# Transposes in the middle of a slice's matmuls, half of each cast of b on VectorE, and a last output piece of 128 columns: what each did to matmul, GELU, matmul

## The chip, the cores and the metric

One core of one Trainium2 chip. The metric is the device time of the whole program in microseconds (us). It holds about 1.8 us that the profiled span doesn't (before: 124.75 us for a span of 123.0 us).

## The reference

```python
h = a @ b                       # a 1024 x 1024, b 1024 x 2048, fp32
h = 0.5 * h * (1 + tanh(sqrt(2 / pi) * (h + 0.044715 * h**3)))
return h @ c                    # c 2048 x 1024
```

## The kernel before

The contraction of the first product runs over k in eight slices of 128. In the opening, six groups of 128 columns of b (the first 768 columns of the tile b_lo; GpSimd loads its other 512 for the next four groups) are multiplied with the first 512 rows of a, slice by slice as the data land. SyncE issues those loads. VectorE (DVE) casts a slice of a to bf16, TensorE (PE) transposes it, DVE copies it out of PSUM, ScalarE (ACT) casts the slice of b.

```python
    nc.gpsimd.tensor_copy(gate, b_st[5][:, 0:1])    # GpSimd waits for b slice 5 before its own loads
    ...
    def mm0(k):
        for t in range(N0):                                   # N0 = 6
            nc.tensor.matmul(ps[t], bt(k, t), aT[0][:, k, :], ...)

    for k in range(KT):                                       # KT = 8
        ab = abf.tile([128, 4, 128], BF16, name="ab")
        nc.vector.tensor_copy(ab, a_st[k])                    # cast of a
        pt = tpool.tile([128, H], BF16, name="pt")
        for j in range(4):
            nc.tensor.transpose(pt[:, ts(j, 128)], ab[:, j, :], ident)
        nc.vector.tensor_copy(aT[0][:, k, :], pt)             # copy of aT
        for i in range(2):
            nc.scalar.activation(b_lo[:, k, ts(i, W0 // 2)], b_st[k][:, ts(i, W0 // 2)], AF.Copy)
        if k > 0:
            mm0(k - 1)                                        # one slice behind the transposes
    mm0(KT - 1)
    ...
    for k in range(0, KT, 4):                                 # the next four column groups
        load_b(k, 4, W0, W1)                                  # GpSimd loads and casts them
        for i in range(4):
            for t in range(N1):
                nc.tensor.matmul(ps[t], bt(k + i, N0 + t), aT[0][:, k + i, :], ...)
    ... # (cut: the rest of both products)
    for q in range(2):                                        # last output row block, two pieces of 256
        w = H // 2
        p = bank(w)
        prod(p, whole(h12), whole(c21), 3, q=ds(q * w, w))
        ot = new_out()
        nc.vector.tensor_tensor(ot[:, 0:w], p, last_keep[:, ds(q * w, w)], op=ADD)
        store(ot, 3, q * w, w)
```

## Time and profile before

124.86 us median of 4 runs (124.63 to 124.98).

| stretch of the profiled run | what sets its end |
|---|---|
| 0 to 17.1 us | landing of a and b |
| 17.1 to 22.1 us | PE: two slices' transposes, three slices' matmuls; and a GpSimd load landing at the same moment |
| 22.1 to 119.6 us | PE, nearly without a gap |
| 119.6 us to the end | an addition, a store of 128 KB, the closing |

The same opening by stretch, from the profile before. The columns are the stretch, its length, then busy us and number of instructions of PE, PE's weight loads, DVE, ACT and GpSimd, the granted clock, the DMA engines' busy share and GB/s.

```profile
10.00:17.00 7.00, 5.99 (x38) 3.07 (x40) 3.22 (x8) 3.75 (x8) 1.33 (x3) 1.00 1.06 378
17.00:22.10 5.10, 4.75 (x28) 2.08 (x27) 1.93 (x4) 2.79 (x6) 4.46 (x7) 1.00 1.12 194
```

DVE is busy for less than half of these stretches and ACT for about half.

### The profile page before, as it was taken

The page shows a single profiled execution, that of the slowest core. Times are in us where ns is not written, and L with a number is a line of the kernel's source. Part 1 is how long each engine was busy: PE and PEld are TensorE (multiplying, and loading weights), DVE is VectorE, ACT ScalarE, POOL GpSimd, SP SyncE. Part 2 cuts the span into 40 slices and gives each one's busy share as a digit, 9 for nine tenths or more (in the row PEclk, how much of TensorE's full clock was granted, in tenths as well). Part 3 has the DMA queues.
Part 4 walks back from the last instruction along what each step waited for, and adds up shares of the span by engine and source line. Part 5 has one row for each costly group of instructions (what it writes and reads, how often), then busy time and mean ns, then how long its engine had stood idle before and what let it go on. Part 6 is the DMA issues. An engine that isn't in the chain of part 4 may idle for free.

```text
span 123.0 us, 1436 instructions
## 1 busy us (share of the span) xinstructions
PE 114.0 (93%) x555; PEld 66.8 (54%) x562; DVE 65.2 (53%) x94; ACT 29.6 (24%) x54; POOL 21.1 (17%) x26
## 2 busy tenths in 40 slices
PE   6955889999998999999999999999999999999990
PEld 2323444444456444444444444468888888888860
DVE  0233533000015200007999999999669999964440
ACT  4034545806331133233323333000000000000000
POOL 2000099133440210000000000995000000000000
PEclk9999999999999999999999999999999999999997
DMA  3899999999999999996000000001500023353433
GB/s 108 198 358 384 379 295 193 205 202 203 212 206 206 316 398 238 206 208 103 0 3 0 5 0 0 0 0 55 201 0 0 5 85 113 143 195 146 171 143 113
DMA packets 14213, 18.43 MB, mean 150 GB/s; under 512 B 768, under 2 KB 9728, under 8 KB 14208
## 3 DMA queue, kind: packets, MB, share of 16 engines
q0 software_dynamic: 7968, 8.91, 39.4%
q1 hardware_dynamic: 6240, 9.44, 22.0%
q8 instruction: 4, 0.07, 0.2%
q14 instruction: 1, 0.01, 0.0%
HBM read 20.97 MB, written 4.19 MB: 205 GB/s over the span
## 4 chain that ended last, share of the span: by engine, by line
PE 82%; DMA 12%; DVE 1%; SPq 1%; issue 1%; DVEq 0%
PE ps L246 41%; PE ps L143 31%; DMA a_st<-in_a_dram 12%; PE ps L102 3%; PE ps L134 3%; PE pt L134 3%; PE pt L162 1%; DVE aT L163 1%; PE pt L110 1%; DVE ab L107 0%; SPq L82 0%; SPq L76 0%; DVE ot L316 0%; DVEq L107 0%
## 5 line engine op out<-in xcount | busy, mean ns | idle before, releaser
L119 ACT ACTIVATE h<-ps 128x512 fp32r<-128x512 f32 (+1 forms) x30 | 17.3, 602 | 27.5 <-PE ps L143 25.2
L143 PE MATMUL ps<-aT,b_hi 128*128 128x512 bf16 x93 | 21.2, 379 | 0.2
L143 PE MATMUL ps<-aT,b_lo 128*128 128x512 bf16 x79 | 17.4, 379 | 0.1
L143 PEld LDWEIGHTS <-b_hi 128*128 128x128 bf16 x96 | 9.3, 98 | 10.8
L246 PE MATMUL ps<-t,s 128*128 128x512 f32 x64 | 15.1, 393 | 0.0
L246 PE MATMUL ps<-t,h 128*128 128x512 f32 x64 | 14.8, 389 | 0.0
L246 PE MATMUL ps<-c,h 128*128 128x512 bf16 (+1 forms) x71 | 14.1, 355 | 0.1
L246 PEld LDWEIGHTS ps<-t,s 128*128 128x128 f32 x64 | 12.0, 188 | 2.6
L246 PEld LDWEIGHTS ps<-t,h 128*128 128x128 f32 x64 | 12.0, 188 | 2.5
L286 POOL COPY lk<-u 128x512 f32<-128x512 f32 x1 | 7.6, 7579 | 33.5 <-ACT u L279 33.5
L143 PEld LDWEIGHTS <-b_lo 128*128 128x128 bf16 x80 | 7.8, 98 | 9.4
L200 DVE TENSOR_TENSOR t<-c,c 128x1024 fp32r<-128x1024 bf16 x4 | 4.7, 1222 | 15.4 <-DMA c<-in_c_dram 15.1
L163 DVE COPY aT<-pt 128x1024 bf16<-128x1024 bf16 x4 | 2.7, 688 | 18.1 <-PE pt L162 18.0
L102 PE MATMUL ps<-aT,b_lo 128*128 128x512 bf16 x47 | 11.5, 379 | 0.1
L246 PEld LDWEIGHTS <-h 128*128 128x128 bf16 x72 | 7.0, 98 | 7.0 <-issue 0.3
L113 ACT ACTIVATE b_lo<-b_st 128x384 bf16<-128x384 f32 x16 | 7.5, 515 | 10.2 <-DMA b_st<-in_b_dram 10.0
L188 POOL DMA_DIRECT2D c<-in_c_dram x8 | 5.9, 743 | 12.3 <-PE ps L143 6.0
L269 DVE TENSOR_TENSOR ot<-ps,u 128x512 f32<-128x512 f32 x11 | 7.3, 682 | 1.1 <-PE ps L246 1.1
L246 PE MATMUL ps<-c,s 128*128 128x512 f32 x32 | 7.4, 389 | 0.0
L107 DVE CAST ab<-a_st 128x512 bf16<-128x512 f32 x8 | 3.7, 463 | 6.0 <-DMA a_st<-in_a_dram 6.0
L246 PEld LDWEIGHTS ps<-c,s 128*128 128x128 f32 x32 | 6.0, 188 | 1.2
L110 PE MATMUL pt<-ident,ab 128*128 128x128 bf16 x32 | 3.2, 223 | 3.7 <-DVE ab L107 3.7
(37 smaller groups left out, 91.4 us busy)
## 6 DMA issues: line engine op xcount, KB each, us to landing
out_dram<-ot SPq DMA_DIRECT2D x15, 256.0 KB, 2.0
b_st<-in_b_dram SPq DMA_DIRECT2D x8, 384.0 KB, 8.6
c<-in_c_dram POOLq DMA_DIRECT2D x6, 512.0 KB, 14.7
c<-in_c_dram POOLq DMA_DIRECT2D x2, 1024.0 KB, 15.0
a_st<-in_a_dram SPq DMA_DIRECT2D x3, 512.0 KB, 8.9
b_hi<-in_b_dram POOLq DMA_DIRECT2D x4, 384.0 KB, 11.2
b_lo<-in_b_dram POOLq DMA_DIRECT2D x2, 512.0 KB, 7.1
ab<-in_a_dram POOLq DMA_DIRECT2D x4, 256.0 KB, 13.8
```

What stands on the lines that cost most here:

```text
L102: nc.tensor.matmul(ps[t], bt(k, t), aT[0][:, k, :], start=(k == 0), stop=(k == KT - 1))
L110: nc.tensor.transpose(pt[:, ts(j, 128)], ab[:, j, :], ident)
L113: nc.scalar.activation(b_lo[:, k, ts(i, W0 // 2)], b_st[k][:, ts(i, W0 // 2)], AF.Copy)
L119: nc.scalar.activation(hq[h][t // NH][:, t % NH, :], p, AF.Gelu_apprx_tanh)
L134: nc.tensor.matmul(ps[t], bt(k + i, N0 + t), aT[0][:, k + i, :], start=(k + i == 0), stop=(k + i == KT - 1))
L143: nc.tensor.matmul(p, bt(k, t), aT[h][:, k, :], start=(k == 0), stop=(k == KT - 1))
L163: nc.vector.tensor_copy(aT[1][:, :, ts(j, 128)], pt)
L188: nc.gpsimd.dma_start(out=dst[:, t:t + 4, :], in_=cv[:, r * NH + t:r * NH + t + 4, ts(q, H)])
L200: nc.vector.tensor_tensor(t1[i], c12[:, ts(i, 2), :], c11[:, ts(i, 2), :], op=SUB)
L246: nc.tensor.matmul(p, lhs(t)[:, ts(j, 128)], rhs(t)[:, q], start=(t == 0), stop=(t == NH - 1))
L269: nc.vector.tensor_tensor(ot, u if swap else p, p if swap else u, op=op)
L286: nc.gpsimd.tensor_copy(last_keep, last)
```

## The change

Its intent: have slice k's matmuls not wait behind slice k+1's transposes, get a b slice ready sooner by sharing its cast between two engines, and make the last addition and store small.

```diff
-    for k in range(KT):
+    def cast_a0(k):
         ab = abf.tile([128, 4, 128], BF16, name="ab")
         nc.vector.tensor_copy(ab, a_st[k])
+        return ab
+
+    def turn0(k, ab):
         pt = tpool.tile([128, H], BF16, name="pt")
         for j in range(4):
             nc.tensor.transpose(pt[:, ts(j, 128)], ab[:, j, :], ident)
         nc.vector.tensor_copy(aT[0][:, k, :], pt)
-        for i in range(2):
-            nc.scalar.activation(b_lo[:, k, ts(i, W0 // 2)], b_st[k][:, ts(i, W0 // 2)], AF.Copy)
-        if k > 0:
-            mm0(k - 1)
-    mm0(KT - 1)
+
+    HW = W0 // 2
+    turn0(0, cast_a0(0))
+    for k in range(KT):
+        nc.vector.tensor_copy(b_lo[:, k, 0:HW], b_st[k][:, 0:HW])
+        nc.scalar.activation(b_lo[:, k, HW:W0], b_st[k][:, HW:W0], AF.Copy)
+        if k + 1 < KT:
+            ab = cast_a0(k + 1)
+        for t in range(N0):
+            nc.tensor.matmul(ps[t], bt(k, t), aT[0][:, k, :], ...)
+            if t == 2 and k + 1 < KT:
+                turn0(k + 1, ab)
...
-    for q in range(2):
-        w = H // 2
+    for q0, w in ((0, 384), (384, 128)):
         p = bank(w)
...
```

More of the change, by code (lines that the diff above doesn't have):

```diff
@@ L98 @@
     ps = [ppool.tile([128, H], F32, name="ps") for _ in range(N0)]
-    def mm0(k):
-        for t in range(N0):
-            nc.tensor.matmul(ps[t], bt(k, t), aT[0][:, k, :],
-                             start=(k == 0), stop=(k == KT - 1))
-    for k in range(KT):
+    def cast_a0(k):
         ab = abf.tile([128, 4, 128], BF16, name="ab")
         nc.vector.tensor_copy(ab, a_st[k])
+        return ab
+    def turn0(k, ab):
         pt = tpool.tile([128, H], BF16, name="pt")
@@ L111 @@
         nc.vector.tensor_copy(aT[0][:, k, :], pt)
-        for i in range(2):
-            nc.scalar.activation(b_lo[:, k, ts(i, W0 // 2)], b_st[k][:, ts(i, W0 // 2)], AF.Copy)
-        if k > 0:
-            mm0(k - 1)
-    mm0(KT - 1)
+    HW = W0 // 2
[6 more added lines that the diff above has]
+        for t in range(N0):
+            nc.tensor.matmul(ps[t], bt(k, t), aT[0][:, k, :],
+                             start=(k == 0), stop=(k == KT - 1))
+            if t == 2 and k + 1 < KT:
+                turn0(k + 1, ab)
     def gelu(t, h, p):
@@ L310 @@
         combine(4 + j, 0, p, u3[:, j, :], op=SUB, swap=True)
-    for q in range(2):
-        w = H // 2
+    for q0, w in ((0, 384), (384, 128)):
         p = bank(w)
-        prod(p, whole(h12), whole(c21), 3, q=ds(q * w, w))
+        prod(p, whole(h12), whole(c21), 3, q=ds(q0, w))
         ot = new_out()
-        nc.vector.tensor_tensor(ot[:, 0:w], p, last_keep[:, ds(q * w, w)], op=ADD)
-        store(ot, 3, q * w, w)
+        nc.vector.tensor_tensor(ot[:, 0:w], p, last_keep[:, ds(q0, w)], op=ADD)
+        store(ot, 3, q0, w)
 _INS = ['a', 'b', 'c']
```

## The prediction

> **What bounds the kernel now.** I read the page's head first, then its chain of work that ended last, then the timeline of the opening and of the end, since the change touches only those two.
>
> ```profile
> span 123.0 us, 1436 instructions
> PE 114.0 (93%) x555; PEld 66.8 (54%) x562; DVE 65.2 (53%) x94; ACT 29.6 (24%) x54; POOL 21.1 (17%) x26
> ...
> PE 82%; DMA 12%; DVE 1%; SPq 1%; issue 1%; DVEq 0%
> ```
>
> PE carries 82% of the chain. The 12% of DMA is the loading of a, up to 17.1 us; after it the chain is PE without a break until one DVE addition at 119.65 us. So a change pays only by what it takes from the first 22 us or from the last 5; the long middle moves as one block, since PE is at 90% or more in nearly every slice of it. The list of waits from 10 to 23 us tells more of the opening:
>
> ```profile
> POOL gate L91 <- DMA b_st<-in_b_dram: 14.4, 1, 14.4
> ACT b_lo L113 <- DMA b_st<-in_b_dram: 4.5, 3, 1.5
> PEld L110 <- DVE ab L107: 3.7, 4, 1.8
> ...
> PE pt L110 <- DVE ab L107: 2.0, 3, 1.3
> ...
> PEld L134 <- DMA b_lo<-in_b_dram: 0.4, 1, 0.4
> ```
>
> PE loses only 2.0 us to the casts of a in that stretch, all of them released by a's DMA. The last line decides this case. L134 is the first matmul group after the opening. It needs columns of b that GpSimd loads, and GpSimd issues that load only when the gate has seen the sixth b slice land. The timeline around it:
>
> ```profile
> 15.67 0.19 POOL L91 COPY gate<-b_st 128x1 f32<-128x1 f32 x1 [14.36 <-DMA b_st<-in_b_dram]
> 15.79 1.62 POOL L126 DMA_DIRECT2D b_lo<-in_b_dram  x2
> ...
> 17.15 0.52 DVE L107 CAST ab<-a_st 128x512 bf16<-128x512 f32 x1 [0.60 <-DMA a_st<-in_a_dram]
> 17.40 2.98 POOL L126 DMA_DIRECT2D b_hi<-in_b_dram  x4
> ...
> 18.50 0.65 DVE L107 CAST ab<-a_st 128x512 bf16<-128x512 f32 x1
> ...
> 19.48 2.75 PE L102 MATMUL ps<-aT,b_lo 128*128 128x512 bf16 x12
> ...
> 22.10 6.59 PEld L134 LDWEIGHTS <-b_lo 128*128 128x128 bf16 x32 [0.36 <-DMA b_lo<-in_b_dram]
> 22.10 0.60 PE L134 MATMUL pt<-aT,b_lo 128*128 128x512 bf16 x2
> ```
>
> The first of the two b_lo loads is issued at 15.79 and takes 6.3 us to land (the least of its two latencies), so at about 22.06. The twelve last opening matmuls begin at 19.48 at a pitch of 0.216 us, so PE could start L134 at 19.48 + 12 x 0.216 = 22.07. PE and DMA are ready within 0.04 us of each other. This is a floor: however much earlier PE ends the opening, L134 can't start before that load has landed.
>
> **What the Trainium skill says.** "VectorE: DVE Perf Modes", section "The perf-mode tier table": an fp32 copy in SBUF runs at two elements a cycle, whereas an operand in PSUM loses the two-port mode. The trace agrees: the 128x512 cast of a takes 0.426 us undisturbed, 512 / 2 / 0.96 GHz = 0.267 plus a fixed 0.159. "SBUF — State Buffer", "Who interferes with whom": such a two-port copy or cast shares a port pair with GpSimd, under an exclusive lock, and GpSimd needs it to write DMA descriptors. The trace agrees as to direction: the casts at 17.15 and 18.50, beside GpSimd's issues, took 0.52 and 0.65 us and not 0.43; they were not held for a whole 0.75 us issue, though. "TensorE: Matmul & The Clock Gate", "Back-to-back issue gap": N / 2.4 + 2.5 ns, which gives 0.056, 0.109 and 0.216 us for 128, 256 and 512 columns. The trace has 0.056 for transposes and 0.216 for the 512-column matmuls; the section also warns of 81 ns for 128 columns with weight loads, which the transposes here, each with its own load, don't show. "DMA: Bandwidth & Descriptors", "Anatomy of one DMA": about 2 us of a small DMA are fixed. The trace has 2.0 us for 256 KB and 1.9 for 128 KB stores.
>
> **The change part by part.**
>
> First, the casts. Before, ACT casts both halves of a b slice in about 0.94 us (two at 0.515). After, ACT and DVE cast one half each. This would bring a slice's last weights 0.43 us sooner after its landing, if DVE were free.
>
> Second, the order. Before, DVE does per slice: cast a(k), copy aT(k). Neither depends on b, and PE does transposes of slice k, then the six matmuls of slice k-1, which had everything long before: 4 x 0.056 + 6 x 0.216 = 1.52 us a slice, the pace seen from 17.73 on. After, DVE does in this order: cast half b(k), cast a(k+1), copy aT(k+1), cast half b(k+1). The copy can run only after the transposes, these stand behind three matmuls of slice k, and these need the DVE half of b(k). So there is a loop through PE and DVE, which I add up from the timeline, per slice:
> - three matmuls: 3 x 0.216 = 0.648
> - first transpose to the start of DVE's copy: 0.425 to 0.43 (10.64 to 11.07 in the timeline)
> - copy to the start of the next cast on DVE: 11.07 to 11.41, 0.342
> - the cast of 384 columns: 384 / 2 / 0.96 GHz = 0.200 + the fixed 0.159 = 0.36 (estimate from the 512-column cast)
> - DVE's end to PE's start: 0.058 (a cast of 10.155 + 0.426 ends at 10.58, its transposes start at 10.64)
>
> Sum 1.83 us, against 1.52 of PE work: 0.3 us of idle PE in each slice, wherever the data are already there.
>
> Where are they? Slices 2 and 3 of a land at 10.13 (the cast at 10.15 waited for it). Transposes at 10.64, copy at 11.07, cast of b(2) at 11.41 to 11.77, so slice 2's matmuls begin at 11.83. From there I step on with the landings of before, read from the ACT casts and a casts that waited for them: b(3) 12.14, a(4) 13.59, b(4) 14.57, b(5) 15.62, a(6) 17.06, b(6) 18.03, b(7) 19.0. Starts of slices 3 to 7 by the loop: 13.67, 15.50, 17.33, 19.17, 21.00. Each b needed has landed before its DVE cast comes up (b(6) at 18.03 for a cast at 18.75, b(7) at 19.0 for 20.58), and each a just before its transposes (a(6): cast 17.2 to 17.7, transposes 17.98). So from slice 2 on the loop sets the pace and not the DMA. Slice 7 ends its six matmuls at 21.00 + 6 x 0.216 = 22.29. That is 0.19 us after the 22.10 of before.
>
> Third, the port. The b casts on DVE at about 16.9, 18.75 and 20.58 are on the loop and fall beside GpSimd's issues, which run from 15.79 to 21.4. The two disturbed casts of before lost 0.09 and 0.22, mean 0.16; three would be up to 0.47. I take 0.3 for it. Opening: about +0.5 us, within 0.2 to 0.7.
>
> Fourth, the end. Before: two pieces of 256 columns, 16 x 0.109 = 1.75 us of PE, then a DVE addition and a store:
>
> ```profile
> 117.69 1.92 PE L246 MATMUL ps<-c,h 128*128 128x256 bf16 x16
> ...
> 118.78 0.42 DVE L316 TENSOR_TENSOR ot<-ps,lk 128x256 f32<-128x256 f32 x1 [0.20 <-PE ps L246]
> 119.65 0.42 DVE L316 TENSOR_TENSOR ot<-ps,lk 128x256 f32<-128x256 f32 x1 [0.45 <-PE ps L246]
> ```
>
> After: 8 x 0.1625 + 8 x 0.056 = 1.75 us, the same. The additions go by 0.69 us for 512 columns and 0.42 for 256, 1.03 ns a column: 0.56 for 384 and 0.29 for 128. Counted from the start of these matmuls, s = 117.69: the first piece is ready at s + 1.51 and added by s + 2.07. The second is ready at s + 1.96, has to wait for DVE until about s + 2.0, and is added by s + 2.3, against s + 2.38 before. But its store stands behind the first piece's on the same queue: that is issued at s + 2.10, takes 0.33 (each store issue here does), and with the queue's own 0.1 between, the last store goes out at s + 2.54, against s + 2.41. Landing takes 1.9 us almost whatever the size. So the smaller last piece gives about +0.1 us, not a gain.
>
> Sum: 124.92 + 0.5 + 0.1 = 125.5 us.
>
> **The rivals.** (1) The opening gets shorter: the halved casts and the transposes in the middle fill PE's waits, since b(6), cast by two engines, could be used from 18.6. For it: those waits are real, 2 us after 10 us. Against: L134 waits for its load until 22.06 anyway. It would make 124.9, and with a good end 124.8. (2) The shared port delays GpSimd: the gate's copy at 15.67 would meet the cast of a(5) or b, the loads go out some 0.3 us later, and all later loads shift. Against: the hardware queue still holds 1.3 MB then and keeps the engines busy until about 18.5, so a late issue is mostly hidden, and PE comes at 22.3 or later by my loop. It would add up to 0.3 us. (3) DMA is the bound of the whole opening and nothing moves: then 124.9 to 125.0, by the end alone. (4) The last store's smaller addition and transfer win: -0.1 us; against it speaks the issue order.
>
> **Range and chances.** With no disturbance at the port, 125.2; with all of it, 125.7; with the second rival, 126.0; if the loop is shorter than I count or hidden behind the load, 124.9. Runs of before spread over 0.35 us. I take 124.9 to 126.0. 2% are 2.5 us, which no part here reaches: slower by over 2% 0.01, faster 0.01.
>
> **What would show it.** In the changed profile: a PE pitch near 1.83 us from slice to slice between 11.8 and 21 us, with PE idle 0.3 us before each slice's first matmul, released by a DVE cast of b_lo; L134's start at 22.3 to 22.8 with its weights no longer waiting for the DMA; everything after it shifted by the same amount; casts of over 0.36 us beside GpSimd; the last store issued 0.1 us later after the last PE group than before. I am wrong if the slices follow at 1.5 us, if L134 starts at 22.1 or sooner (then the opening was only waiting on its load), or if that load lands far from 22.06.

## The result, and the profile after

125.42 us median of 4 runs (125.27 to 125.76) against 124.86; ratio 1.0052, 95% interval 1.0026 to 1.0077. A ratio is the mean time of one kernel's fast runs over that of the other's fast runs of the same rounds, so not quite the ratio of the medians. The change makes the kernel half a per cent slower, inside the 2% that count as the same.

The changed kernel's page and, below the dots, its list of waits from 10 to 23 us (who waited for whom: us in all, times, longest):

```profile
span 123.5 us, 1438 instructions
PE 84%; DMA 6%; DVE 5%; SPq 2%; issue 1%; DVEq 0%
...
PEld L119 <- DVE b_lo L114: 4.1, 6, 1.0
...
PE ps L119 <- DVE b_lo L114: 0.5, 1, 0.5
```

The DMA share of the chain went from 12% to 6%, DVE's from 1% to 5%. The loads didn't become faster: the chain of the opening now runs through DVE, where it ran through the loads. L119 is the opening's matmul (L102 before), L114 DVE's cast of half a b slice. Six times the weights of a slice's first matmul waited for that cast. Here is that part of the chain in order of time (start, us, what):

```profile
11.86 0.82 PE ps L119 x3
12.68 0.24 PE pt L108 x4
12.92 0.02 issue
12.94 0.42 DVE aT L109
13.37 0.28 DVE b_lo L114
13.64 0.05 issue
13.69 0.82 PE ps L119 x3
...
15.52 0.82 PE ps L119 x3
16.34 0.24 PE pt L108 x4
16.58 0.02 issue
16.60 0.42 DVE aT L109
17.03 0.60 DVE b_lo L114
17.63 0.05 issue
17.68 0.82 PE ps L119 x3
...
19.51 0.82 PE ps L119 x3
...
21.34 1.47 PE ps L119 x6
```

One turn is three matmuls, four transposes, DVE's copy, DVE's cast, and PE again. The turns start at 11.86, 13.69, 15.52, 17.68, 19.51 and 21.34: 1.83 us apart, except for one of 2.16. The long one contains a cast of 0.60 us in the chain where the others have 0.28. GpSimd was issuing a load at that time; the first line below is from a query for GpSimd alone, the others are of the timeline:

```profile
16.69 0.75 POOL L132 DMA_DIRECT2D b_lo<-in_b_dram  x1
...
15.12 0.35 DVE L114 CAST b_lo<-b_st 128x384 bf16<-128x384 f32 x1
...
16.95 0.68 DVE L114 CAST b_lo<-b_st 128x384 bf16<-128x384 f32 x1
...
22.43 0.74 PEld L140 LDWEIGHTS <-b_lo 128*128 128x128 bf16 x4
22.64 0.59 PE L140 MATMUL pt<-aT,b_lo 128*128 128x512 bf16 x2
```

L140 is the first matmul group after the opening (L134 before). It starts at 22.64 and not 22.10, and no wait for a DMA stands behind its weights now: PE itself came too late. So the opening cost 0.54 us. Of it, 0.33 is the one long turn (2.16 - 1.83), and the remaining 0.21 the five turns' pace together with data that landed 0.04 us later in this run.

The end of the changed kernel, timeline first, then its two last stores as the page's list of DMA issues has them (KB each, us to landing):

```profile
118.19 1.92 PE L252 MATMUL ps<-c,h 128*128 128x384 bf16 x16
...
119.70 0.76 DVE L321 TENSOR_TENSOR ot<-ps,lk 128x384 f32<-128x384 f32 x2 [0.63 <-PE ps L252]
...
out_dram<-ot SPq DMA_DIRECT2D x1, 192.0 KB, 2.0
out_dram<-ot SPq DMA_DIRECT2D x1, 64.0 KB, 1.7
```

The last PE group starts 0.50 us later than before (118.19 against 117.69), so the middle passed on nearly all of the 0.54. From there, the two additions end after 119.70 + 0.76 - 118.19 = 2.27 us, against 119.65 + 0.42 - 117.69 = 2.38 before; the last store goes out later because the larger one is ahead of it, but lands in 1.7 us where the 128 KB took 1.9. The spans differ by 0.5 us, as the opening does; nothing is left for the end.

### The profile page after: what moved, and what is told of

Same layout as the page of the kernel before. It is cut to its first block, busy times and chain, and to the rows that moved or that the text cites. A ratio compares the mean times of both kernels' runs of the same rounds, so it can differ in the third digit from the quotient of the medians.

```text
span 123.5 us, 1438 instructions
## 1 busy us (share of the span) xinstructions
PE 115.5 (94%) x562; PEld 66.2 (54%) x562; DVE 67.4 (55%) x102; ACT 26.3 (21%) x46; POOL 21.0 (17%) x26
## 4 chain that ended last, share of the span: by engine, by line
PE 84%; DMA 6%; DVE 5%; SPq 2%; issue 1%; DVEq 0%
PE ps L252 40%; PE ps L149 31%; DMA a_st<-in_a_dram 6%; PE ps L119 5%; PE pt L140 3%; PE ps L140 3%; DVE aT L109 2%; DVE b_lo L114 2%; PE pt L108 1%; PE pt L168 1%; SPq L82 1%; SPq L76 1%; DVE aT L169 1%; DVE ab L102 0%; DVEq L347 0%
## 5 line engine op out<-in xcount | busy, mean ns | idle before, releaser
L149 PE MATMUL ps<-aT,b_lo 128*128 128x512 bf16 x80 | 17.4, 379 | 0.0
L119 PE MATMUL ps<-aT,b_lo 128*128 128x512 bf16 x48 | 12.9, 381 | 2.1 <-DVE b_lo L114 1.3
L252 PE MATMUL ps<-c,h 128*128 128x512 bf16 (+2 forms) x72 | 14.2, 355 | 0.0
L149 PEld LDWEIGHTS <-b_lo 128*128 128x128 bf16 x80 | 7.8, 98 | 9.4
L119 PEld LDWEIGHTS <-b_lo 128*128 128x128 bf16 x48 | 3.7, 97 | 7.9 <-DVE b_lo L114 5.8
L109 DVE COPY aT<-pt 128x512 bf16<-128x512 bf16 x8 | 3.4, 425 | 6.7 <-PE pt L108 6.7
L115 ACT ACTIVATE b_lo<-b_st 128x384 bf16<-128x384 f32 x8 | 4.2, 524 | 13.1 <-DMA b_st<-in_b_dram 13.1
```

Source lines behind the costliest of these rows:

```text
L115: nc.scalar.activation(b_lo[:, k, HW:W0], b_st[k][:, HW:W0], AF.Copy)
L119: nc.tensor.matmul(ps[t], bt(k, t), aT[0][:, k, :], start=(k == 0), stop=(k == KT - 1))
L149: nc.tensor.matmul(p, bt(k, t), aT[h][:, k, :], start=(k == 0), stop=(k == KT - 1))
L252: nc.tensor.matmul(p, lhs(t)[:, ts(j, 128)], rhs(t)[:, q], start=(t == 0), stop=(t == NH - 1))
```

## The experiments

All gave correct results. "Before" is the kernel before in the same rounds. One run of before in the rounds of before_gate4 took 243.98 us and is left out of the ratio. late_gate ran once, so its state is unknown.

| run | this, median us | before, median us | ratio, 95% interval |
|---|---|---|---|
| open_only | 125.39 | 124.79 | 1.0050, 1.0016 to 1.0084 |
| end_only | 124.70 | 124.79 | 0.9985, 0.9953 to 1.0017 |
| act_casts_b | 124.59 | 124.79 | 0.9975, 0.9934 to 1.0017 |
| b_cast_first | 125.22 | 124.79 | 1.0029, 0.9988 to 1.0070 |
| late_gate | 129.22 (one look) | 124.76 | none |
| old_order_dve_b | 125.15 | 124.76 | 1.0022, 0.9990 to 1.0054 |
| act_split_load | 124.45 | 124.76 | 0.9968, 0.9932 to 1.0003 |
| first_split_load | 125.22 | 124.76 | 1.0029, 0.9986 to 1.0073 |
| after_again | 125.11 | 124.67 | 1.0041, 1.0019 to 1.0062 |
| act_again | 124.91 | 124.67 | 1.0020, 0.9987 to 1.0052 |
| act_gate4 | 123.77 | 124.67 | 0.9940, 0.9917 to 0.9963 |
| before_gate4 | 124.81 | 124.83 | 0.9995, 0.9944 to 1.0046 |

Theory: the loss is in the opening, 0.2 us of it a loop between PE and DVE that the order of DVE's work makes, the rest casts that GpSimd holds up. Rivals: the end costs; the transposes in the middle cost by themselves; it is the amount of DVE's work; the load after the opening is the bound whatever is done.

**open_only and end_only: which half carries the loss?** Each is one part of the change alone.

```diff
 # open_only: the changed kernel with
-    for q0, w in ((0, 384), (384, 128)):
+    for q0, w in ((0, 256), (256, 256)):
 # end_only: the kernel before with the changed loop over (0, 384), (384, 128)
```

> The change's opening with the old end (two pieces of 256 columns). If the whole loss comes from the loop through PE and DVE in the opening, this run carries all of it: 0.4 to 0.6 us over the kernel before, slices of the opening 1.83 us apart, the one b cast beside GpSimd's loads stretched, and the first matmul after the opening at 22.5 to 22.7 us and not 22.1. If the end is what costs, it is within 0.1 us of before.

> The old opening with the new end (384 and 128 columns). The opening theory expects a difference from before within 0.1 us: in the changed kernel the last store went out 0.11 us later after the start of the last PE group but landed 0.13 us faster. The rival that the end costs expects +0.1 us or more; the one that a small last piece pays expects -0.1 us or more.

The opening alone gave the whole loss (1.0050, the change as a whole 1.0052), with the first matmul after it at 22.47 us, a little short of the 22.5 to 22.7 expected: its stretched cast lost 0.14 us (0.49 against 0.35). The end alone can't be told from nothing (0.9985). That rival falls.

**late_gate: the loop without GpSimd's issues.**

```diff
-    nc.gpsimd.tensor_copy(gate, b_st[5][:, 0:1])
+    nc.gpsimd.tensor_copy(gate, b_st[7][:, 0:1])
```

> The changed kernel with GpSimd's gate on the eighth b slice and not the sixth, so that no GpSimd load is issued before about 19 us. The port theory: the VectorE casts up to then, the b casts at about 17 and 19 us above all, are undisturbed (0.35 us for 384 columns, 0.42 for 512), and the slices follow at 1.83 us each without the one of 2.16. The loop alone is then seen: the last opening slice starts at about 21.0 and ends at about 22.3 us. If the stretched cast had another cause than GpSimd, it comes back. The load that follows is late on purpose (it lands at 23 to 24 us), so the whole is 0.5 to 1.5 us slower than the changed kernel; its total tells nothing.

```profile
16.69 0.35 DVE L114 CAST b_lo<-b_st 128x384 bf16<-128x384 f32 x1
16.95 0.42 DVE L102 CAST ab<-a_st 128x512 bf16<-128x512 f32 x1
...
18.52 0.35 DVE L114 CAST b_lo<-b_st 128x384 bf16<-128x384 f32 x1
18.78 0.42 DVE L102 CAST ab<-a_st 128x512 bf16<-128x512 f32 x1
...
20.35 0.65 DVE L114 CAST b_lo<-b_st 128x384 bf16<-128x384 f32 x1
```

The casts that fell beside issues in the changed kernel are undisturbed here, and the casts of b follow at 1.83 us (16.69, 18.52, 20.35). GpSimd's issues begin at 19.19, and the one cast after that is stretched to 0.65. So the stretching moved with GpSimd, and the pace of 1.83 us stayed: two separate causes. The run also gave something that it was not made for. In the stretches of this run, after the last b slice has landed:

```profile
19.20:20.50 1.30, 1.30 (x10) 0.57 (x8) 0.50 (x3) 0.12 (x1) 1.30 (x3) 1.00 0.00 0
20.50:22.00 1.50, 1.06 (x6) 0.48 (x6) 0.50 (x1) 0.52 (x2) 1.50 (x3) 1.00 0.62 55
22.00:24.80 2.80, 0.52 (x3) 0.03 (x1) 0.00 (x0) 2.53 (x6) 2.80 (x5) 0.99 1.24 204
```

The DMA engines stand still (share 0.00) for 1.3 us after the issue at 19.19 and then come up slowly; the load lands 5.6 us after its issue with nothing queued ahead of it. In the kernel before it was 6.3 us, and in the other profiles with this load unsplit 5.6 to 6.8. A GpSimd load's landing is thus set by its issue and not mainly by what is queued ahead of it. The total was 3.8 us over the changed kernel's 125.42 and not 0.5 to 1.5 as I had expected. Two lines show why:

```profile
24.86 1.04 PE L140 MATMUL pt<-aT,b_lo 128*128 128x512 bf16 x2 [2.34 <-DMA b_lo<-in_b_dram]
...
24.80:28.30 3.50, 3.44 (x9) 1.29 (x10) 0.00 (x0) 0.00 (x0) 0.60 (x2) 0.52 1.27 205
```

L140 started at 24.86 and not 22.64, 2.2 us later. PE had then been idle for 2.34 us, and its granted clock was 0.52 in the stretch that followed: the next eight matmuls came 0.40 to 0.43 us apart and not 0.216, another 1.6 us. After the wait of 0.80 us in act_again (below) they came 0.22 us apart at once.

**act_casts_b and act_again: both halves of b on ScalarE, transposes still in the middle.**

```diff
-        nc.vector.tensor_copy(b_lo[:, k, 0:HW], b_st[k][:, 0:HW])
+        nc.scalar.activation(b_lo[:, k, 0:HW], b_st[k][:, 0:HW], AF.Copy)
```

> The changed kernel, but ScalarE casts both halves of each b slice again; the transposes stay in the middle of the matmuls. The loop theory: no b cast stands behind the copy of aT on VectorE any more, so a slice costs three matmuls 0.65, 0.425 to the copy, the copy 0.424 and 0.06 to PE, 1.56 us, or the 1.52 us of PE work; the last opening slice ends at about 21.5 us, and the first matmul after it starts when its load has landed (21.6 to 22.1). So at or below the kernel before by 0 to 0.5 us, and 0.5 to 1.0 us under the changed kernel. A rival that the transposes in the middle themselves cost (PE's order, not VectorE's) expects it to stay 0.3 us or more slower than before.

> The kernel with both b halves on ScalarE and the transposes in the middle, again: 0.2 to 0.4 us under before (124.59 and 124.45 with the load split were measured, each within noise of before), 0.6 to 0.9 us under the changed kernel. If its first run was luck of early loads, it is level with before.

The two runs have 0.9975 and 1.0020, both level with before within their intervals. So the transposes in the middle aren't what costs; with DVE's half undone the loss is gone or mostly gone. But the gain that I expected is not there either (act_again is 0.24 us over before by the medians, not 0.2 to 0.4 under), and the second profile shows why:

```profile
19.68 1.70 PE L119 MATMUL ps<-aT,b_lo 128*128 128x512 bf16 x7
22.18 0.61 PE L140 MATMUL pt<-aT,b_lo 128*128 128x512 bf16 x2 [0.80 <-DMA b_lo<-in_b_dram]
```

The opening's matmuls end at 19.68 + 1.70 = 21.38, and PE then stands idle for 0.80 us for the load. In the profile of act_casts_b the load happened to land 1 us sooner after its issue (5.6 us against 6.6), no such wait was there, and L140 started at 20.92: that single run had 123.53 us. Why the load's time varies so from run to run is not known.

**act_gate4 and before_gate4: the load issued earlier.** Both move the gate by one slice, the first on the kernel of act_casts_b, the second on the kernel before.

```diff
-    nc.gpsimd.tensor_copy(gate, b_st[5][:, 0:1])
+    nc.gpsimd.tensor_copy(gate, b_st[4][:, 0:1])
```

> The same with GpSimd's gate on the fifth b slice. With the gate on the eighth, the first load took 5.6 us from issue to landing on engines that had nothing else to do, so its landing follows its issue: here it is issued about 1 us earlier (14.3 to 14.6) and lands at 19.8 to 20.6, clear of the first matmul after the opening. But its packets then share the engines with the last a and b slices, which land 0 to 0.5 us later. If the load was still a floor, 0.1 to 0.4 us faster than with the gate on the sixth; if the last b slice is the bound, 0 to 0.5 us slower.

> The kernel before with nothing changed but GpSimd's gate on the fifth b slice. In two profiles with its opening, PE was ready for the first matmul behind the load at 22.07 and 21.73 us and started within 0.04 us of that, so an earlier load has little to gain: 0 to 0.3 us under before. Then the 0.9 us of the version with both b halves on ScalarE, transposes in the middle and this gate need both, PE's new order and the earlier load. If the gate alone brings 0.6 us or more, PE's order had no part in it.

act_gate4 is 0.6% faster than before, the only gain clear of noise, and the fastest kernel; it beats both kernels. Against act_again it gained 1.14 us by the medians, where 0.1 to 0.4 was expected. In its profile L140 follows the opening at once, at 20.98 us:

```profile
19.69 1.46 PE L119 MATMUL ps<-aT,b_lo 128*128 128x512 bf16 x6
20.98 0.59 PE L140 MATMUL pt<-aT,b_lo 128*128 128x512 bf16 x2
```

The last b slices didn't land later for it. The gate alone, on the kernel before, gives nothing (0.9995): in the profile of before PE is ready at 22.07 and the load lands at 22.06, and in that of before_gate4, where a and b landed some 0.6 us later, the load was there at 21.99 and PE ready only at 22.73. Two things end at about the same time, and to move one of them shows no gain. The wait for the load was real as a floor, and PE's new order has a worth of its own once the floor is lowered and DVE is kept out of the loop.

**b_cast_first: DVE keeps half of b, but casts b(k+1) ahead of the copy of aT(k+1).**

```diff
-    turn0(0, cast_a0(0))
-    for k in range(KT):
+    def cast_b0(k):
         nc.vector.tensor_copy(b_lo[:, k, 0:HW], b_st[k][:, 0:HW])
         nc.scalar.activation(b_lo[:, k, HW:W0], b_st[k][:, HW:W0], AF.Copy)
+
+    turn0(0, cast_a0(0))
+    cast_b0(0)
+    for k in range(KT):
         if k + 1 < KT:
             ab = cast_a0(k + 1)
+            cast_b0(k + 1)
```

> The changed kernel with VectorE still casting half of each b slice, but its cast of b(k+1) placed ahead of the copy of aT(k+1) and not behind it. If the order on VectorE makes the loop, the pitch falls from 1.83 to about 1.56 us where the data are there, the last slice ends at about 21.7 us, and the time is that of the kernel before or up to 0.4 us less. If it is the mere amount of work on VectorE, or the port it shares with GpSimd, that costs, it stays 0.3 to 0.6 us over before.

Its time is undecided (1.0029, with 1 inside the interval), so my expectation of a gain was missed; by the medians it is 0.43 us over before, where the expectation had put the rival of DVE's work and the port. In its trace the loop's regular waits are gone, but the floor is there:

```profile
22.86 0.11 PEld L144 LDWEIGHTS <-b_lo 128*128 128x128 bf16 x2 [1.00 <-DMA b_lo<-in_b_dram]
22.86 0.39 PE L144 MATMUL pt<-aT,b_lo 128*128 128x512 bf16 x1 [0.51 <-DMA b_lo<-in_b_dram]
```

The floor itself came later here: the gate's copy on GpSimd, beside a cast of b on DVE, took 0.37 us and not 0.19, and the load was issued 0.37 us after the sixth b slice had landed (16.42 after 16.05), against 0.17 in before. That is the prediction's second rival at work; first_split_load shows the same (0.37 and 0.36 us).

**act_split_load and first_split_load: that load in four pieces.** On the kernels of act_casts_b and b_cast_first.

```diff
-    for k in range(0, KT, 4):
-        load_b(k, 4, W0, W1)
-        for i in range(4):
+    for k in range(0, KT, 2):
+        load_b(k, 2, W0, W1)
+        for i in range(2):
```

> The kernel with both b halves on ScalarE and the transposes in the middle, whose first matmul after the opening stood 0.16 us after its load's landing, with GpSimd's two loads of 512 columns split into four of half the rows. The first quarter lands about 1.3 us sooner after the last b slice, so the load isn't a floor any more: the first matmul after the opening follows the last opening matmul at once, at about 2.5 us after the last b slice's landing. Faster than before by 0.3 to 0.7 us; against the unsplit one 0 to 0.3 us. If the load was never the floor, it is the same as the unsplit one.

> The kernel with VectorE's b cast ahead of the copy, in whose trace the first matmul after the opening stood idle for 0.51 us for its load, with that load split in the same way. The floor theory: that idle time goes, and it comes to 0.2 us above to 0.3 below the kernel before, 0.3 to 0.5 us less than unsplit. If GpSimd's stretching of the casts and not the load is its limit, it stays 0.2 to 0.4 us above before.

The idle time at the end of the opening went in both profiles, but neither time is clear of before's, and first_split_load didn't get faster at all. Part of the gain turned into a new wait, since two more issues push GpSimd's later loads back (those of b_hi are issued from 18.50 on, against 17.12 in act_again). In act_split_load:

```profile
29.51 0.39 PE L149 MATMUL ps<-aT,b_hi 128*128 128x512 bf16 x1 [0.36 <-DMA b_hi<-in_b_dram]
```

**old_order_dve_b: the old order on PE, DVE casting half of b.**

```diff
-        for i in range(2):
-            nc.scalar.activation(b_lo[:, k, ts(i, W0 // 2)], b_st[k][:, ts(i, W0 // 2)], AF.Copy)
+        nc.vector.tensor_copy(b_lo[:, k, 0:HW], b_st[k][:, 0:HW])
+        nc.scalar.activation(b_lo[:, k, HW:W0], b_st[k][:, HW:W0], AF.Copy)
```

> The kernel before, its order on PE kept (transposes of slice k ahead of the matmuls of slice k-1), with VectorE casting half of each b slice behind the copy of aT. The loop theory: here the cast of b(k) has the whole of slice k-1's matmuls to finish in, so it is on no loop, PE goes at 1.52 us a slice where data are there, and the time is that of before within 0.2 us. The rival that more work on VectorE beside GpSimd costs by itself expects 0.3 us or more over before.

Between the two (1.0022, undecided; by the medians 0.39 us over before and so outside the 0.2 that the loop theory allowed). The loop isn't there, but its trace has a stretched cast of b in front of a cast of a that PE needs:

```profile
18.22 0.58 DVE L113 CAST b_lo<-b_st 128x384 bf16<-128x384 f32 x1
18.72 0.41 DVE L107 CAST ab<-a_st 128x512 bf16<-128x512 f32 x1
19.18 0.23 PEld L110 LDWEIGHTS <-ab 128*128 128x128 bf16 x4 [0.54 <-DVE ab L107]
```

So the rival of DVE's amount of work isn't refuted for a part of the loss: beside GpSimd, more casts on DVE are more casts to be held up, in any order.

**after_again: the changed kernel once more.**

> The changed kernel itself once more, beside the next two on the same chip, because single runs spread by 0.4 us. Loop and port together: 0.4 to 0.7 us over before, of it 0.19 from the loop and 0.1 to 0.4 from stretched VectorE casts beside GpSimd's loads; at least one b or a cast between 16 and 21 us takes 0.5 us or more.

0.44 us over before by the medians; the opening's turns again at 1.83 us with one of 2.13, whose cast of b took 0.65. In these rounds the three kernels stand side by side: 125.11 as changed, 124.91 with DVE's half undone, 123.77 with the earlier gate as well.

**All profiles side by side.** The last b slice lands between 18.39 and 19.61 us from profile to profile, so the time at which PE is through with the opening is better counted from that landing: 3.07 to 3.12 us in the three profiles of the old opening, 3.46 to 3.64 in the three of the changed one (3.58 in late_gate), 2.66 and 2.76 with the cast ahead of the copy, 2.49 to 2.53 in the four with both halves on ScalarE, and 3.29 in old_order_dve_b. So with the same work on DVE, the place of its cast makes 0.7 us or more, and the work itself 0.1 to 0.3 in the new order and 0.2 in the old. PE's new order with both halves on ScalarE is ready 0.6 us sooner than before; the loop took more than that away, and without the loop the load took it.

## Why the prediction was right

The time (125.5 predicted, 125.42 measured) and its main mechanism were right. That the sum came so close is partly luck: 0.5 for the opening and 0.1 for the end stand against 0.54 and nothing. By its steps:

- **The loop: right, in size too.** The sum of five durations from the trace of before gave 1.83 us; the traces of after, late_gate and after_again have 1.83. Slice 2 was to start at 11.83 and started at 11.86. The cast of 384 columns, estimated at 0.36, took 0.35.
- **The port: right in the total, off in its make-up.** The prediction had three casts that lose 0.16 each on average, and took 0.3. In the trace one cast of b lost 0.33 and the two others nothing; in open_only one lost 0.14, in after_again one 0.30. The total hit by luck: which cast is held, and for how long, depends on where in a GpSimd issue it starts (last section).
- **The floor: right as a mechanism, wrong as a fixed time.** "At about 22.06" was one run's landing. In the profile after it was 21.60 (issued at 15.81), in act_again 22.13. So one of the prediction's own signs of being wrong, a landing far from 22.06, did come, but without effect: PE was later still. That the first matmul can't start before it, act_again and act_gate4 showed. The first rival, a gain from PE's side, was thus rightly turned down for this change, and is what act_gate4 collects.
- **The end: mis-sized.** Expected +0.1 us; the last store did go out later, but the term "landing takes 1.9 us almost whatever the size" was wrong: 64 KB took 1.7, 128 KB 1.9, 256 KB 2.0. That gives the 0.1 back, and end_only is level.
- **The argument against the second rival was wrong.** It said that a late GpSimd issue is hidden behind 1.3 MB in the hardware queue. late_gate showed the same load taking 5.6 us with nothing queued, so a late issue would have moved the landing. It did no harm only because GpSimd's first issue was not late: 15.81 against 15.79. In b_cast_first and first_split_load it was.

Open: why the load's time from issue to landing differs by up to 1.2 us between runs (5.6 to 6.8), and how much b_cast_first would gain with the earlier gate.

## What to carry to other kernels

An engine's idle share doesn't tell whether it can take more work: write down the order of its instructions and look for a loop through another engine (here PE, copy, cast, PE), and add up one turn from the trace. Where an engine and a load become ready at the same moment, only moving both shows a gain; read each one's own time before judging a change by the total.

## What the Trainium skill lacked or had wrong

- "SBUF — State Buffer", "Who interferes with whom": the port pair is said to be held "for the whole instruction", while the other "fully blocks". For GpSimd's DMA issues (about 0.75 us each) the runs show a part of it only. A DVE cast that starts some 0.26 to 0.54 us into an issue of this length is held until about 0.54 to 0.61 us into it, in all the profiles. Start in the issue plus stretch: before 18.50 - 18.13 + (0.65 - 0.42) = 0.60; after 16.95 - 16.69 + (0.68 - 0.35) = 0.59; late_gate 20.35 - 20.07 + (0.65 - 0.35) = 0.58. A cast that starts 0.12 us into one isn't stretched (after, 19.10 in an issue of 18.98: 0.35 us), and then the issue can be the longer one: 0.83 us where DVE's cast came at 17.54 into an issue of 17.42. Longer issues fit less well: a cast 0.29 us into one of 1.01 us (act_gate4, 14.55) isn't held, one 0.50 us into one of 0.88 us (open_only, 17.23) is held until 0.68. That an issue takes the pair only about a quarter of a us in, and who asks first wins as the page says, would fit most of this but isn't shown.
- "DMA: Bandwidth & Descriptors", "Anatomy of one DMA": 2.0 us plus bytes / 436e3 gives 4.4 us for 1 MB. The casting load here (1 MB read, 512 KB written) took 5.6 us with nothing queued ahead of it (late_gate), 6.3 in before and 6.6 in act_again. A second load was issued 0.88 us behind it each time, so no run times one alone, and whether casting has a price of its own stays open. The section is about loads that GpSimd issues; SyncE's stores took 1.7 us for 64 KB, 1.9 for 128 KB and 2.0 for 256 KB.
- "TensorE: Matmul & The Clock Gate", "Back-to-back issue gap": the sustained 131 ns for 512 columns and 81 ns for 128 columns with weight loads were not seen. The section's other formula, which it gives for isolated matmuls, held in sustained streams, each matmul with its own weight load: 0.216 us for 512 columns, and 0.056 us for 128 in the transposes and in the last output piece.
